# Splitting the pooling and delta branch inputs inside the last attention batch of a two-layer hybrid decoder step

## The chip, the cores and the metric

The kernel runs on one core of one Trainium2 chip. The metric is device microseconds (us) of one execution of the whole program, median of three runs. A core has five engines that take their instructions in order and wait for each other through semaphores: PE (the matrix multiplier TensorE), DVE (VectorE), ACT (ScalarE), POOL (GpSimd) and SP (SyncE), which here only issues transfers from main memory. In the trace, PEld is PE's load of the stationary operand, which runs beside its matmuls.

## What is computed

Two layers of a decoder; 256 prompt tokens and 8 sample rows of 8 tokens, so 320 token columns, with a cached past of 2048 positions for each sample row. What matters here, cut from the reference:

```python
y_a = y_pool * silu(z_pool)               # causal pooling, 512 channels
o_lat = _mla_attend(q_lat, q_rope, keys_lat, keys_rope, pos, k_pos)
o_mla = einsum('blhc,chd->blhd', o_lat, w_uv).reshape(B, L, MLA_WIDTH)
y_b = o_mla * silu(z_mla)                 # attention, 512 channels
y_c = _rmsnorm(o_dn, dn_norm_g) * silu(z_dn)   # gated delta rule, 512 channels
gates = sigmoid(h_gate).reshape(B, L, N_BRANCH, D_MODEL)
merged = (gates[:, :, 0] * (y_a @ w_br_pool) + gates[:, :, 1] * (y_b @ w_br_mla)
          + gates[:, :, 2] * (y_c @ w_br_dn))
x = x + merged @ w_out                    # 1024 -> 1024
```

## The kernel before

Everything is held channels by tokens: a tile is 128 channels by 320 columns. Products in full precision are done as three fp32r matmuls: a weight tile is loaded into `wraw` (four buffers, SP's queue), ACT copies its high half to `wh` (L196), DVE subtracts to get the low half `wl` (L197), and `mm3` multiplies high by high (L220), high by low (L221) and low by high (L222) for each block of 128 input channels. The activations are split in the same way: `yH` by ACT (L202), `yL` by DVE (L203). The inputs of the three branches stand in `zs`: entries 0 to 3 pooling, 4 to 7 attention, 8 to 11 delta. A branch product `br` for one of eight output blocks m is 4 blocks of input channels, so 12 matmuls; a gate product `gate` has 8 blocks, so 24. In the text, product (n, m) is branch n (0 pooling, 1 the delta branch, 2 attention, in the order in which the loops run) and output block m. The table `branches` in the code holds, for each n, the gate number, the weight and the first entry of `zs`.

A layer goes through its projections, convolutions and the delta rule (with a triangular solve, L760 to L770, on DVE), then attention over the cached past of the sample rows, one row (batch, `bb`) after another, then the branch products, and `w_out` (`wo`). In the loop over `bb`, a batch takes the scores `sc` (PE, L1166), softens them (DVE maximum L1185, ACT exponential L1196), runs a gate product on PE beside that, combines the batch before (`olat`), transposes the weights (`PT` for the past, `PTn` for the own tokens), multiplies them with the cached values (`attend`: 32 `pv` matmuls L1237 and the own part L1241), and scales the result into `o` on ACT (L1243). The loop stands in a manual schedule: PE, DVE, ACT and POOL run it in the order in which it is written. All that stands behind the loop is placed by the compiler's automatic scheduler, which may move it forward into the loop's last batches; SP's transfers are always placed by it.

Behind the loop stand the split of the pooling branch (`split_y(p3a, 0)`, the last line in the manual schedule), product (0, 0), the last combination, in the second layer the last gate product, product (0, 1), and `oml`, which multiplies the combined attention by `w_uv`. Then the pools of the attention are closed, the pool `p3` opens, the delta and attention inputs are split (L202, L203), the residual `xT` is loaded (POOL queue, L1449, 1280 KB), and the other 22 products run by pairs of output blocks, each followed by its use: `acc` (L1327) for branch 0, `gt` (L1329) and a sum on POOL (L1330) for the two others. Gate results that were put aside in main memory come back on POOL's queue (L1316). In PSUM, the attention has four banks of the tag A, which `gate`, `olat`, `PT`, `PTn`, `pv`, `br` and `oml` take in turn: a matmul into a bank waits until the bank's last reader is done.

Of the kernel before, what the change touches and what calls it, by code (L numbers as in the profile page):

```python
# [11 lines left out]
F32 = mybir.dt.float32  # L12
F32R = mybir.dt.float32r
I32 = mybir.dt.int32
AF = mybir.ActivationFunctionType
# [4 lines left out]
DM, TP, TS, T = 1024, 256, 64, 320  # L20
# [96 lines left out]
def trunk(tc, I, O, layers=2):  # L117
# [292 lines left out]
    for l in range(layers):  # L410
# [896 lines left out]

        def split_y(pool, y0):
            yb[y0] = (pool.tile([128, 4, T], F32R, name=f"yH{y0}"), pool.tile([128, 4, T], F32R, name=f"yL{y0}"))
            for i in range(4):  # L1310
                split_x(yb[y0][0][:, i, :], yb[y0][1][:, i, :], zs[y0 + i])

        def branch(n, m, tag):
            if (n, m) in spilled:
                t = per.tile([128, T], F32, tag="gt", name="gt", bufs=NG)
                nc.gpsimd.dma_start(t, spilled[n, m])  # L1316
            else:
                if (n, m) not in early:
                    gate("pj")
                t = early[n, m]  # L1320
            _, wname, y0 = branches[n]
            w = split_w(load_w(I[wname][l][:, m * 128 : m * 128 + 128], 4, 128)[:, :4, :], 4)
            b = ps(tag, "br")
            mm3(b[:, :T], w, yb[y0], 4)
            if n == 0:
                accs[m] = p3a.tile([128, T], F32, tag="acc", name="acc", bufs=4)
                stt(accs[m], t, 1.0, b[:, :T], add, mult)  # L1327
            else:
                stt(t, t, 1.0, b[:, :T], add, mult)  # L1329
                nc.gpsimd.tensor_tensor(accs[m], accs[m], t, add)  # L1330


        with tc.manual_schedule(engines={mybir.EngineType.PE, mybir.EngineType.DVE, mybir.EngineType.Activation, mybir.EngineType.Pool}):
# [18 lines left out]
            for h in range(11):  # L1352
# [20 lines left out]
                if 3 <= h < 8:  # L1373
                    flip(0, keys, parts_[h - 3])
            phc.close()
            pb = pbc.enter_context(tc.tile_pool(name=f"pb_{l}", bufs=1, side="right", reuse_waits="tile"))
            gs = [gate_w() for _ in range(GL[0])]
# [4 lines left out]
            for bb in range(NB):  # L1382
                more = bb + 1 < NB
                S = soften(bb, sc, mx)
                if more:
# [4 lines left out]
                if more:  # L1390
                    flip(bb + 1, keys, 1)
                g = [(gs[0][0], gate_mm("A", gs[0][1]))]
                if o is not None:
# [11 lines left out]
                if two:  # L1405
                    gate_mm("A", gs[1][1], b, (4, 8))
                    gate_out(gs[1][0], b, bb < 6)
                weigh(bb, mx)
                o = attend(bb, PT, PTn, mx)
                if more:  # L1410
# [6 lines left out]
            wuv = load_wuv(pb.tile([128, 1024], F32, tag="S", name="wuv", bufs=2))  # L1417
            pdc.close()
            p3e = ExitStack()
            p3a = p3e.enter_context(tc.tile_pool(name=f"p3a_{l}", bufs=1, reuse_waits="tile"))  # L1420
            yb = {}
            split_y(p3a, 0)
        branch(0, 0, "A")
        combined(NB - 1, combine(o))
        if order:
            gate("A")
        branch(0, 1, "A")
        b = ps("A", "oml")
# [5 lines left out]
        for p in range(4):  # L1434
            stt(zs[4 + p][:, TP:], b[:, p * 64 : p * 64 + 64], 0.5, zs[4 + p][:, TP:], mult, mult)
        pbc.close()
        p2b.close()
        p2c.close()
        pec.close()


        last = l == layers - 1
        p3c, p3 = enter(f"p3_{l}", dict(pj=2, A=6) if last else dict(pj=4, A=4))
        wcfg.update(pool=p3, n=2)
        split_y(p3, 8)
        split_y(p3, 4)
# [3 lines left out]
        for mp in range(4):  # L1450
            for n in range(3):
                for m in (2 * mp, 2 * mp + 1):
                    if n or m > 1:
                        branch(n, m, "A")
# [74 lines left out]
```

## Times and profile before

| what | value |
|---|---|
| time, median of 3 runs (lowest, highest) | 1063.83 us (1061.71, 1064.25) |
| the profiled execution's own time | 1066.27 us |
| its span, first to last instruction | 1064.5 us |
| mean granted TensorE clock | 0.962 |
| PE, DVE, ACT, POOL busy | 995.7, 725.8, 456.5, 338.0 us |
| end of attention, first layer (last batch's scores to the eighth branch product) | 446 to 479 us |
| the same of the second layer | 964 to 995 us |
| triangular solve of the second layer | 627 to 646 us |

A row of the timeline gives the start and duration of an instruction (or of a run of like ones, xN), its engine, line, tiles, and in brackets how long the engine had been idle and what it waited for. The durations are of the profiled execution. Matmuls overlap each other: the distance between their starts is what one costs.

### The profile page before, as it was taken

Reading aid. Unit: us, or ns where it says so; the run is one execution under the profiler, and the core shown is the slowest. Engines: PE = TensorE matmul, PEld = TensorE weight load, DVE = VectorE, ACT = ScalarE, POOL = GpSimd, SP = SyncE. Lnnn points to the kernel's source line nnn. Section 1 sums busy time; section 2 is a strip of 40 time slices with the busy share of each in tenths; the row PEclk is TensorE's granted clock in tenths of the full one; section 3 lists DMA queues with packets and bytes.
Section 4 is the critical chain, followed back from the end, with each engine's and each line's share of the span. In section 5 each row is a group of like instructions: output and inputs, shape, how many; then the busy total and the mean of one; then the engine's idle time right before and its main releaser. Section 6 shows DMA issues by size and latency. Waiting matters only on the chain.

```text
span 1064.5 us, 24733 instructions
## 1 busy us (share of the span) xinstructions
PE 995.7 (94%) x10179; PEld 866.4 (81%) x10179; DVE 725.8 (68%) x1387; ACT 456.5 (43%) x810; POOL 338.0 (32%) x469
## 2 busy tenths in 40 slices
PE   8988899999979999989989979999998899999996
PEld 6877798987857888779978868999876678777996
DVE  3999884558676666558748988656666657574872
ACT  5663353543433333334545624336344333334453
POOL 3666221215151101025445542211335211100641
PEclk8999899999989999999998989999998899999998
DMA  8532333733645776258663332355255376742961
GB/s 231 155 97 80 100 92 84 206 95 106 190 139 158 237 242 222 96 154 233 158 200 79 101 99 70 101 153 141 71 162 182 102 254 211 248 157 83 278 169 50
DMA packets 202697, 159.22 MB, mean 150 GB/s; under 512 B 27704, under 2 KB 191826, under 8 KB 200010
## 3 DMA queue, kind: packets, MB, share of 16 engines
q1 hardware_dynamic: 176364, 98.47, 34.1%
q0 software_dynamic: 7424, 48.75, 13.0%
q10 hardware_dynamic: 18798, 10.44, 3.4%
q8 instruction: 80, 1.31, 0.5%
q14 instruction: 31, 0.25, 0.1%
HBM read 144.17 MB, written 13.68 MB: 148 GB/s over the span
## 4 chain that ended last, share of the span: by engine, by line
PE 71%; DVE 15%; ACT 5%; issue 3%; DMA 3%; POOL 1%; ACTq 0%; SPq 0%; DVEq 0%; POOLq 0%
PE sc L1166 6%; PE pv L1237 5%; PE gate L220 5%; PE pj L220 5%; PE pj L222 5%; PE gate L222 4%; PE pj L221 4%; PE gate L221 4%; DVE cy L505 4%; PE br L220 3%; PE br L221 2%; DVE wl L197 2%; PE br L222 2%; PE wo L220 2%; PE wo L222 2%
## 5 line engine op out<-in xcount | busy, mean ns | idle before, releaser
L196 ACT ACTIVATE wh<-wraw 128x1024 fp32r<-128x1024 f32 (+1 forms) x180 | 166.4, 935 | 174.3 <-PE pj L221 93.0
L197 DVE TENSOR_TENSOR wl<-wraw,wh 128x1024 fp32r<-128x1024 f32 (+2 forms) x165 | 187.9, 1147 | 69.2 <-ACT wh L196 68.2
L220 PE MATMUL pj<-xnH,wh 128*128 128x320 f32 (+1 forms) x528 | 174.7, 331 | 13.5 <-DVE V L497 7.6
L222 PE MATMUL pj<-xnH,wl 128*128 128x320 f32 (+1 forms) x528 | 172.3, 326 | 6.7 <-DVE wl L197 6.4
L221 PE MATMUL pj<-xnL,wh 128*128 128x320 f32 (+1 forms) x528 | 170.0, 322 | 0.0
L220 PE MATMUL gate<-xnH,wh 128*128 128x320 f32 x384 | 124.7, 325 | 1.5 <-DVE V L497 1.5
L222 PE MATMUL gate<-xnH,wl 128*128 128x320 f32 x384 | 120.5, 314 | 1.8 <-DVE wl L197 1.3
L220 PEld LDWEIGHTS pj<-xnH,wh 128*128 128x128 f32 (+1 forms) x528 | 103.4, 196 | 21.1 <-ACT wh L196 6.9
L221 PE MATMUL gate<-xnL,wh 128*128 128x320 f32 x384 | 119.4, 311 | 0.0
L222 PEld LDWEIGHTS pj<-xnH,wl 128*128 128x128 f32 (+1 forms) x528 | 103.1, 195 | 11.6 <-DVE wl L197 7.8
L221 PEld LDWEIGHTS pj<-xnL,wh 128*128 128x128 f32 (+1 forms) x528 | 103.3, 196 | 3.2 <-issue 1.8
L220 PEld LDWEIGHTS gate<-xnH,wh 128*128 128x128 f32 x384 | 72.8, 190 | 9.6 <-issue 6.3
L1156 DVE STREAM_TRANSPOSE KT<-kv 128x1024 f32<-128x1024 f32 x64 | 78.6, 1228 | 0.6
L222 PEld LDWEIGHTS gate<-xnH,wl 128*128 128x128 f32 x384 | 72.7, 189 | 3.3 <-DVE wl L197 1.8
L221 PEld LDWEIGHTS gate<-xnL,wh 128*128 128x128 f32 x384 | 72.8, 190 | 1.1 <-issue 0.8
L220 PE MATMUL br<-yH,wh 128*128 128x320 f32 x192 | 60.3, 317 | 5.7 <-ACT wh L196 1.9
L1237 PE MATMUL pv<-kv,PT 128*64 128x256 f32 x512 | 58.8, 382 | 2.3 <-ACT PT L1215 2.3
L1166 PE MATMUL sc<-KT,q 32*64 32x256 f32 x2048 | 59.9, 380 | 0.0
L221 PE MATMUL br<-yL,wh 128*128 128x320 f32 x192 | 59.6, 313 | 0.0
L222 PE MATMUL br<-yH,wl 128*128 128x320 f32 x192 | 59.1, 313 | 0.0
L505 DVE SCALAR_TENSOR_TENSOR cy<-V,prm,cy 128x344 f32<-128x344 f32 x72 | 56.5, 804 | 0.5
L1166 PEld LDWEIGHTS sc<-KT,q 32*64 32x64 f32 x2048 | 45.8, 132 | 12.7 <-issue 6.2
(406 smaller groups left out, 2055.2 us busy)
## 6 DMA issues: line engine op xcount, KB each, us to landing
wraw<-in_w_in SPq DMA_DIRECT2D x114, 512.0 KB
wraw<-in_w_out SPq DMA_DIRECT2D x16, 512.0 KB
q<-q4d SPq DMA_DIRECT2D x64, 72.0 KB
gate<-gt ACTq DMA_DIRECT2D x28, 160.0 KB
gt<-gate POOLq DMA_DIRECT2D x28, 160.0 KB, 3.6
wraw<-in_w_br_pool SPq DMA_DIRECT2D x16, 256.0 KB
wraw<-in_w_br_dn SPq DMA_DIRECT2D x16, 256.0 KB
wraw<-in_w_br_mla SPq DMA_DIRECT2D x16, 256.0 KB
```

The costliest lines, as they stand in the source:

```text
L196: act(h, raw, AF.Copy)
L197: (nc.gpsimd.tensor_tensor if spare or turn[0] in K["lo"] else tt)(lo, raw, h.bitcast(F32), sub)
L220: nc.tensor.matmul(out, wh[:, k, :], xh[:, first + k, :], start=k == 0, stop=False)
L221: nc.tensor.matmul(out, wh[:, k, :], xl[:, first + k, :], start=False, stop=False)
L222: nc.tensor.matmul(out, wl[:, k, :], xh[:, first + k, :], start=False, stop=k == nk - 1)
L505: stt(y, V[:, j : j + 344], wj(j), y, mult, add)
L1156: nc.vector.transpose(v[:, a], kv[:, a * 1024 : a * 1024 + 1024].rearrange("p (i k c) -> p i k c", i=4, k=8))
L1166: nc.tensor.matmul(sc[64 * hf : 64 * hf + 64, g, :256], q4[r, k, :], krT[r, keys_] if k == 8 else KT[r, k, keys_], start=k == 0, stop=k == 8,)
L1237: nc.tensor.matmul(pv[64 * hf : 64 * hf + 64, :256], PT[:, n * 128 + 64 * hf : n * 128 + 64 * hf + 64], kv[:, r : r + 256], start=n == 0, ...
```

## The change

The pool `p3a` opens at the start of the last batch (bb = 7), and ACT copies the high halves of the pooling inputs there, before the batch's exponential; DVE takes the low halves after its maximum, and the weight of product (0, 0) is split behind that. Product (0, 0) runs between the transposes and `attend`, and before `attend` the weight of (0, 1) and the delta inputs are split as well. Behind the loop, and now within the manual schedule, come the use of (0, 0), in the second layer the last gate product, (0, 1), the combination, the weights of both delta products, product (1, 0); then `oml` and (1, 1). Four products are then done when `p3` opens, where two were; `branch` is cut in three functions for it. The attention inputs are split in `p3` as before.

```diff
@@ -1305,29 +1305,47 @@
-        def split_y(pool, y0):
+        yb = {}
+
+        def split_hi(pool, y0):
             yb[y0] = (pool.tile([128, 4, T], F32R, name=f"yH{y0}"), pool.tile([128, 4, T], F32R, name=f"yL{y0}"))
             for i in range(4):
-                split_x(yb[y0][0][:, i, :], yb[y0][1][:, i, :], zs[y0 + i])
-
-        def branch(n, m, tag):
+                act(yb[y0][0][:, i, :], zs[y0 + i], AF.Copy)
+
+        def split_lo(y0):
+            for i in range(4):
+                tt(yb[y0][1][:, i, :], zs[y0 + i], yb[y0][0][:, i, :].bitcast(F32), sub)
+
+        def split_y(pool, y0):
+            split_hi(pool, y0)
+            split_lo(y0)
+
+        def branch_w(n, m):
+            wname = branches[n][1]
+            return split_w(load_w(I[wname][l][:, m * 128 : m * 128 + 128], 4, 128)[:, :4, :], 4)
+
+        def branch_mm(n, w, tag):
+            b = ps(tag, "br")
+            mm3(b[:, :T], w, yb[branches[n][2]], 4)
+            return b
+
+        def branch_out(n, m, b):
...
+        def branch(n, m, tag):
+            if (n, m) not in spilled and (n, m) not in early:
+                gate("pj")
+            branch_out(n, m, branch_mm(n, branch_w(n, m), tag))
...
@@ -1381,6 +1400,11 @@
             o = None
             for bb in range(NB):
                 more = bb + 1 < NB
+                if not more:
+
+                    pdc.close()
+                    p3a = p3e.enter_context(tc.tile_pool(name=f"p3a_{l}", bufs=1, reuse_waits="tile"))
+                    split_hi(p3a, 0)
                 S = soften(bb, sc, mx)
...
                 softened(bb, S, mx)
                 if more:
                     flip(bb + 1, keys, 1)
+                else:
+                    split_lo(0)
+                    w00 = branch_w(0, 0)
                 g = [(gs[0][0], gate_mm("A", gs[0][1]))]
...
+                if not more:
+                    b00 = branch_mm(0, w00, "A")
                 weigh(bb, mx)
+                if not more:
+                    w01 = branch_w(0, 1)
+                    split_y(p3a, 8)
                 o = attend(bb, PT, PTn, mx)
...
             wuv = load_wuv(pb.tile([128, 1024], F32, tag="S", name="wuv", bufs=2))
-            pdc.close()
-            p3e = ExitStack()
-            p3a = p3e.enter_context(tc.tile_pool(name=f"p3a_{l}", bufs=1, reuse_waits="tile"))
-            yb = {}
-            split_y(p3a, 0)
-        branch(0, 0, "A")
-        combined(NB - 1, combine(o))
-        if order:
-            gate("A")
-        branch(0, 1, "A")
+            branch_out(0, 0, b00)
+            if order:
+                gate("A")
+            b01 = branch_mm(0, w01, "A")
+            combined(NB - 1, combine(o))
+            w10 = branch_w(1, 0)
+            branch_out(0, 1, b01)
+            w11 = branch_w(1, 1)
+            branch_out(1, 0, branch_mm(1, w10, "A"))
         b = ps("A", "oml")
...
+        branch_out(1, 1, branch_mm(1, w11, "A"))
         pbc.close()
...
+        early_br = {(0, 0), (0, 1), (1, 0), (1, 1)}
...
-        split_y(p3, 8)
         split_y(p3, 4)
...
-                    if n or m > 1:
+                    if (n, m) not in early_br:
                         branch(n, m, "A")
```

What this does to PE's order at the end of the first layer's last batch: `PTn` is the last transpose, `pv` the products with the cached values, `br` a branch product, `olat` the last combination. Before:

```order
L1214 MATMUL PT<-cst,S 128x128 x8
L1223 MATMUL PTn<-cst,so 64x64
L1237 MATMUL pv<-kv,PT 64x256 x16
L1241 MATMUL pv<-cko,PTn 64x256
L220 MATMUL br<-yH_5293,wh 128x320
L1249 MATMUL olat<-cst,o 128x64 x2
L220 MATMUL br<-yH_5293,wh 128x320
```

and in the changed kernel, from the last matmuls of product (0, 0) to the first of (0, 1):

```order
L220 MATMUL br<-yH_5209,wh 128x320
L221 MATMUL br<-yL_5210,wh 128x320
L222 MATMUL br<-yH_5209,wl 128x320
L1237 MATMUL pv<-kv,PT 64x256 x16
L1241 MATMUL pv<-cko,PTn 64x256
L220 MATMUL br<-yH_5209,wh 128x320
L221 MATMUL br<-yL_5210,wh 128x320
```

A whole product now stands ahead of the `pv` matmuls, and the next follows them at once. On DVE, in the same batch, from the maximum to the copy of `PTn`, before:

```order
L1195 TENSOR_SCALAR mx<-mx 128x1
L1253 COPY olat<-olat 128x16x8
L460 TENSOR_TENSOR gt<-gate,rn 128x320
L197 TENSOR_TENSOR wl<-wraw,wh 128x512
L1224 COPY PTn<-PTn 64x64
```

and changed:

```order
L1195 TENSOR_SCALAR mx<-mx 128x1
L1317 TENSOR_TENSOR yL_5210<-zs,yH_5209 128x320 x4
L197 TENSOR_TENSOR wl<-wraw,wh 128x512
L1253 COPY olat<-olat 128x16x8
L460 TENSOR_TENSOR gt<-gate,rn 128x320
L1224 COPY PTn<-PTn 64x64
```

Four low halves and a weight's low half now stand ahead of the copy of `olat` and of the reading of the gate's bank (L460). On ACT, at the end of the second layer's last batch, where the last gate's weight is the tile of 1024 columns, before:

```order
L1197 ACTIVATE so,mx<-so,mx 64x64
L196 ACTIVATE wh<-wraw 128x1024
L461 ACTIVATE gt<-gt 128x320
L1215 ACTIVATE PT<-PT 128x512 x2
L1243 ACTIVATE o<-pv,mx 128x256
L202 ACTIVATE yH_11246<-zs 128x320 x4
```

and changed:

```order
L1197 ACTIVATE so,mx<-so,mx 64x64
L196 ACTIVATE wh<-wraw 128x512
L461 ACTIVATE gt<-gt 128x320
L1215 ACTIVATE PT<-PT 128x512 x2
L196 ACTIVATE wh<-wraw 128x512
L1313 ACTIVATE yH_11259<-zs 128x320 x4
L1243 ACTIVATE o<-pv,mx 128x256
L196 ACTIVATE wh<-wraw 128x1024
```

The last gate's weight is split behind `o` now, where the automatic scheduler had put it ahead of the transposes' copies. One more place has moved without a line of the diff on it: the automatic schedule of the second layer's opening, around its triangular solve. DVE there, before (X and R are steps of the solve, `z` and `U` read projections):

```order
L760 STREAM_SHUFFLE X_7137<-R 128x160
L761 TENSOR_TENSOR X_7137<-X_7137,a_6580 128x20x5
L762 TENSOR_TENSOR R<-R,X_7137 128x20x5
L760 STREAM_SHUFFLE X_7141<-R 128x160
L761 TENSOR_TENSOR X_7141<-X_7141,a_6580 128x20x6
L654 TENSOR_TENSOR z<-pj,rn 128x320
L762 TENSOR_TENSOR R<-R,X_7141 128x20x6
L760 STREAM_SHUFFLE X_7145<-R 128x160
```

and changed:

```order
L760 STREAM_SHUFFLE X_7137<-R 128x160
L654 TENSOR_TENSOR z<-pj,rn 128x320
L761 TENSOR_TENSOR X_7137<-X_7137,a_6580 128x20x5
L762 TENSOR_TENSOR R<-R,X_7137 128x20x5
L197 TENSOR_TENSOR wl<-wraw,wh 128x1024
L760 STREAM_SHUFFLE X_7141<-R 128x160
L657 SCALAR_TENSOR_TENSOR th<-th,z 128x320
L761 TENSOR_TENSOR X_7141<-X_7141,a_6580 128x20x6
L762 TENSOR_TENSOR R<-R,X_7141 128x20x6
L760 STREAM_SHUFFLE X_7145<-R 128x160
L626 TENSOR_TENSOR U<-pj,rn 128x256
```

The reading `z` of a projection stands two steps of the solve earlier, and the reading `U` of the next projection stands ahead of the solve's last step instead of behind its end.

## Rows read from the trace of the kernel before

**Rows 1.** Timeline of PE, end of the first layer's attention: start us, us, instruction.

```profile
450.88 0.24 PE L1223 MATMUL PTn<-cst,so 64*64 64x64 f32 x1
451.84 3.67 PE L1237 MATMUL pv<-kv,PT 128*64 128x256 f32 x32 [0.71 <-ACT PT L1215]
...
457.01 0.42 PE L220 MATMUL br<-yH,wh 128*128 128x320 f32 x1 [0.92 <-ACT yH L202]
...
464.81 0.41 PE L220 MATMUL br<-yH,wh 128*128 128x320 f32 x1 [1.92 <-DVE yL L203]
```

**Rows 2.** Timeline of DVE, same stretch.

```profile
450.32 0.48 DVE L460 TENSOR_TENSOR gt<-gate,rn 128x320 f32<-128x320 f32 x1
450.72 0.68 DVE L197 TENSOR_TENSOR wl<-wraw,wh 128x512 fp32r<-128x512 f32 x1
...
467.13 1.70 DVE L203 TENSOR_TENSOR yL<-zs,yH 128x320 fp32r<-128x320 f32 x4
```

**Rows 3.** Timeline of ACT, same stretch.

```profile
448.19 1.15 ACT L1196 ACTIVATE S<-S,mx 128x1024 f32<-128x1024 f32 x1 [4.84 <-DVE mx L1195]
...
449.91 0.63 ACT L196 ACTIVATE wh<-wraw 128x512 fp32r<-128x512 f32 x1
...
456.50 1.54 ACT L202 ACTIVATE yH<-zs 128x320 fp32r<-128x320 f32 x4
```

**Rows 4.** Timelines of SP and POOL (issues of loads), and of ACT behind them.

```profile
451.43 0.37 SPq L176 DMA_DIRECT2D wraw<-in_w_br_mla  x1
463.31 1.50 SPq L176 DMA_DIRECT2D wraw<-in_w_br_pool  x2
```

```profile
463.65 0.53 POOL L1449 DMA_DIRECT2D xT<-xs  x1
```

```profile
472.60 2.19 ACT L196 ACTIVATE wh<-wraw 128x512 fp32r<-128x512 f32 x4 [5.88 <-DMA wraw<-in_w_br_pool]
```

**Rows 5.** Slices: length, busy of PE, PEld, DVE, ACT, POOL, clock, DMA share, GB/s.

```profile
454.00:455.00 1.00, 1.00 (x13) 0.66 (x10) 0.00 (x0) 0.00 (x0) 0.00 (x0) 1.00 0.01 2
```

```profile
475.00:476.00 1.00, 1.00 (x6) 1.00 (x5) 1.00 (x2) 0.00 (x0) 0.70 (x2) 0.50 0.72 215
```

**Rows 6.** The page's part on DMA issues: KB each, us from issue to landing.

```profile
gt<-gate POOLq DMA_DIRECT2D x28, 160.0 KB, 3.6
```

**Rows 7.** Timeline of PE, the end of the sixth to the end of the eighth product.

```profile
471.80 0.31 PE L222 MATMUL br<-yH,wl 128*128 128x320 f32 x1
473.81 0.42 PE L220 MATMUL br<-yH,wh 128*128 128x320 f32 x1 [1.70 <-ACT wh L196]
...
479.07 0.31 PE L222 MATMUL br<-yH,wl 128*128 128x320 f32 x1
```

**Rows 8.** Timelines of PE, ACT and DVE, end of the second layer's attention.

```profile
974.77 0.42 PE L220 MATMUL br<-yH,wh 128*128 128x320 f32 x1 [0.92 <-ACT yH L202]
...
981.11 1.20 PE L1433 MATMUL oml<-olat,wuv 128*64 128x64 f32 x32
...
994.73 0.31 PE L220 MATMUL br<-yH,wh 128*128 128x320 f32 x1
```

```profile
967.65 1.06 ACT L196 ACTIVATE wh<-wraw 128x1024 fp32r<-128x1024 f32 x1
```

```profile
973.89 0.47 ACT L1243 ACTIVATE o<-pv,mx 128x256 f32<-128x256 f32 x1 [3.85 <-PE pv L1241]
```

```profile
968.75 1.23 DVE L197 TENSOR_TENSOR wl<-wraw,wh 128x1024 fp32r<-128x1024 f32 x1 [0.21 <-ACT wh L196]
```

**Rows 9.** Timelines of DVE and PE, triangular solve of the second layer.

```profile
639.06 0.49 DVE L654 TENSOR_TENSOR z<-pj,rn 128x320 f32<-128x320 f32 x1 [1.06 <-PE pj L222]
...
642.10 2.19 DVE L768 TENSOR_TENSOR TS<-R,cst 128x512 f32<-128x512 f32 x3
644.22 0.41 DVE L626 TENSOR_TENSOR U<-pj,rn 128x256 f32<-128x256 f32 x1
```

```profile
645.52 1.00 PE L793 MATMUL Y<-TS,ATm 64*64 64x32 f32 x28 [0.88 <-DVE TS L770]
```

More of the change, by code (lines that the diff above doesn't have):

```diff
@@ L1317, in branch @@
             else:
-                if (n, m) not in early:
-                    gate("pj")
                 t = early[n, m]
[L1321 to L1324, printed above, removed]
             if n == 0:
@@ L1375, in trunk @@
             phc.close()
+            p3e = ExitStack()
             pb = pbc.enter_context(tc.tile_pool(name=f"pb_{l}", bufs=1, side="right", reuse_waits="tile"))
```

## The prediction

> **What bounds the kernel now.** I read the table of engines first, then the list of what PE waits for, stretch by stretch, then the timelines of PE, ACT and DVE side by side around the places the change touches. PE is busy for most of the span, and nearly all branch products follow each other without a gap: 48 matmuls lie between 464.81 [rows 1] and 471.80 [rows 7], 0.146 us each, so a product of 12 costs 1.76 and a gate of 24 costs 3.5. Where PE works like this, moving a product gains nothing. Only waits can be won, and a wait that is won in one place may come back behind it. In the first layer PE waits 0.92 for the first pooling high half and 1.92 for the delta low halves [rows 1], then 1.70 for a weight split [rows 7]. After that last wait the granted clock was half, 0.50 or 1.2 GHz, for about three slices [rows 5]; after the 1.92 it was not. In the second layer the 0.92 is there again [rows 8], and the other two are nearly gone. So the change has most to win in the first layer.
>
> **First layer, ahead of the `pv` products.** ACT's four high halves take 1.54 [rows 3]. They go into its idle 4.84 before the exponential [rows 3]: cost nothing, since PE is on the scores and the gate, and if the cover were gone the exponential would be up to 1.5 late. DVE's four low halves take 1.70 and a weight's low half 0.68 [rows 2]. DVE ends its maximum at about 448.1, so the low halves end at 449.8; ACT's `wh` ends at 450.5 as before [rows 3], and DVE's `wl` at about 451.3. Only then come the copy of `olat` and L460, which before ended at 450.80 [rows 2] and now ends at about 452.0. What is queued behind it on DVE is the copy of `PTn`; who waits is PE, since `PTn` takes the bank that L460 reads. So `PTn` starts at 452.05 instead of 450.88 [rows 1], the 12 matmuls of product (0, 0) run to 454.0, and `pv` starts there, 2.16 later than 451.84 [rows 1] for 1.76 of work moved ahead: a loss of 0.4, the price of the DVE order. The wait of 0.71 for the copies of `PT` is hidden under the product.
>
> **First layer, behind them.** Before, PE was through `pv` at 456.09, which is 457.01 less its wait of 0.92 [rows 1], 4.25 after `pv` began. Now that is 458.25. Product (0, 1) follows at once, because its inputs are there, and covers the scaling of `o`; it ends at 460.0. `olat` takes 0.4 and `oml` 1.2 [rows 8] with some 0.2 for the copy between them, and the two delta products take 3.5, so PE is through four products at 465.4. Before, 24 matmuls from 464.81 [rows 1] ended at 468.3. The lead is 2.9.
>
> Next is the attention branch, whose first matmul needs a bank that is free only when DVE has used product (1, 1), and this use stands on DVE behind the low half of the third pooling weight. That weight's load can be issued when DVE has split the first delta weight, at about 461.4, where before its pair was issued from 463.31 [rows 4]. Uncaught, a load of this size takes about 2.6: the one issued at 451.43 [rows 4] had moved by 454, when the DMA share falls to 0.01 [rows 5]. The page gives 3.6 for a smaller load on POOL's queue [rows 6]. With `wh` 0.63, `wl` 0.68 and the use 0.48 [rows 2, 3], PE goes on between 465.8 and 467.0. I take 467.0, since the residual `xT` is loaded at the same time and so the 3.6 is the nearer row: a wait of 1.6. Four products more are 7.0, and I leave 0.6 for the fourth pooling weight: the layer's 96th branch matmul ends at 474.6. Before, it began at 479.07 [rows 7] and ended at 479.2. From there PE runs without waits, so the lead is kept. **Gain 4.6.** Ends: 5.8 if the load takes 2.6, and 2.7 if the clock falls after the new wait, as follows.
>
> What a fall of the clock costs is in rows 7: 24 matmuls from 473.81 to 479.2 took 5.4 where 3.5 is the price at full clock, so 1.9. The wait in question is a little shorter than the 1.70 that was followed by a fall and than the 1.92 that was not [rows 1, 7]; I take none. The Trainium skill, page "TensorE: Matmul & The Clock Gate", section Part 1 on the clock gate, says that a monitor of PE's activity halves the clock of an idle engine and gives it back to a busy one. The trace agrees after the 1.70, with its 0.50, and shows nothing of it after the 1.92. With a fall after both new waits, this one and the second layer's, the whole sum below would be +3.0; with none after either, −0.8.
>
> **Second layer, end of attention.** The delay of 0.4 on DVE is the same. The removed wait is 0.92 [rows 8]. New is the last gate: before, its weight was split beside the transposes (`wh` 1.06 from 967.65, `wl` 1.23 from 968.75 [rows 8]) and cost PE nothing. Now ACT splits it behind `o`, which itself starts when `pv` is done and takes 0.47 [rows 8]. PE has nothing else in its order there, since the next instruction is the gate's first: it waits 0.47 + 1.06 and about 0.25 of hand-over, 1.8, does two matmuls, and waits about 1.0 more for the low half. From 974.77 to the 96th branch matmul at 994.73 [rows 8] there are 20.1 us for 96 + 24 matmuls (17.6), `oml` (1.2) and `olat` (0.4), so 0.9 of small waits, which the earlier inputs may remove. That makes 1.8 + 1.0 + 0.4 − 0.92 − 0.9 = 1.4 lost. Two idle stretches of together 2.8, close to each other, are more than the 1.70 before the one fall I can see here, so I add 1.9. **Loss 3.3**, ends 1.4 and 4.2 (none of the 0.9 won).
>
> **Second layer, opening.** No line of the diff stands here, but the order has moved, and DVE runs in order. Before, DVE was idle 1.06 until the projection for `z` was there at 639.06 [rows 9]. Now `z` stands two steps of the solve earlier, so those steps wait for the same projection instead of running before it, and `U`, which read its projection at 644.22 [rows 9], behind the solve's end, now stands ahead of its last step. TS, three instructions of 2.19 that began at 642.10 [rows 9], then begin at about 646.7, and `Y`, which waits for them through two transposes, at 650.1 instead of 645.52 [rows 9]: 4.6 later. What PE is given in between is 22 projection matmuls and a transpose, 3.5 us that stood behind `Y` before. If all that follows is bound by PE, 1.1 is lost; if it hangs on `Y`, 4.6; and if the solve's end is waited for elsewhere anyway, nothing. PE waits for DVE here (0.88 before `Y` [rows 9]), so it is not PE alone: I take 2.4. **Loss 2.4**, ends 0 and 4.6.
>
> **The sum.** −4.6 + 3.3 + 2.4 = +1.1 on the profiled execution's 1066.27: 1067.4. The median of the runs shown is 2.4 below that execution, so 1064.9. Other moves (transfer issues one product earlier, pools that open earlier) lie beside PE's work.
>
> **Rivals.** *Faster.* The solve's new order costs nothing because its fillers are needed soon anyway, the load comes in 2.6 (gain 5.8), and the clock holds at the last gate (loss 1.4): −4.4, 1059.4. For it: the scheduler gives PE work in the gap. Against it: three things have to go well at once. Chance 0.14.
>
> *Slower by a caught load.* The third pooling weight's load shares the transfer engines with `xT`, 1280 KB, issued on POOL's queue at 463.65, 0.3 after the pair's issue began [rows 4]; the splits of the pair came at 472.60 [rows 4], 9.3 after it. If that happens to the load now, the wait before the attention branch grows to about 7 us, product eight ends at about 479.4, and the first layer wins nothing: 3.3 + 2.4 = +5.7, 1069.5. It decides if the load's data has not moved before `xT` starts. Against it: `xT` waits for `oml`, so it starts a microsecond or more after the load's issue. Chance 0.17. The Trainium skill, page "DMA: Bandwidth & Descriptors", section Queues, rings and completion order, says that a transfer engine takes turns between its queues, a packet at a time; with turns of equal bytes the load would take twice its 2.6, and the sum would be +2.7, but the 9.3 shows much less than an equal share.
>
> *Slower by the solve.* The opening costs its full 4.6 and the clock falls also after the first layer's new wait (gain 2.7): 4.6 + 3.3 − 2.7 = +5.2, 1069.0. For it: DVE's chain is what PE waits for there. Chance 0.14.
>
> **How the numbers follow.** My forecast has 0.55; its own range is 1061.4 to 1066.9. About 0.3%, 3.2 us, is what a measurement of this kernel can tell from no change; the forecast lies inside it. So faster 0.14, same 0.55, slower 0.31. The range leaves out about 0.1 at each end: 1060.2 to 1069.6.
>
> **What would show it.** Right: no wait of PE for `yH` or delta `yL` in the first layer, `pv` some 2.2 later and (0, 1) directly behind it; a wait of 1.5 or less at the first attention product; PE idle twice on `wh` and `wl` of the last gate in the second layer, with a clock near 0.5 behind; `Y` of the second solve further from the layer's start by some 2 to 5 us. Wrong: a gate weight that is split in time after all, a load that comes after 470, or a solve whose `Y` is not later.

## The result, and the profile after

The changed kernel takes 1071.43 us (median of 5 runs, 1070.81 to 1072.89); the kernel before took 1064.04 beside it (5 runs, 1061.71 to 1066.63). The ratio is 1.0073 with the interval 1.0057 to 1.0089: slower by about 7.4 us, outside the predicted range. A second set of runs on another chip gave 1.0056 (1.0038 to 1.0073).

The profiled execution of after took 1071.43, that of before 1066.27, so 5.2 lie between the two traces. Measured from span start, the first layer's 96th branch matmul begins 3.6 earlier than before, the first `Y` of the second layer's solve 0.5 later, and the second layer's first `wo` matmul 5.3 later (its 96th branch matmul 4.9). The start of the program (no change there) accounts for −0.15 of the first. So the first layer's end won 3.4, 3.1 of it behind the last `sc`; the opening of the second layer lost 4.1; and its end lost 4.7, of which 4.2 lie ahead of the 96th branch matmul.

Busy times are those of before within 4 us (share of the span, instructions):

```profile
PE 998.9 (93%) x10179; PEld 868.5 (81%) x10179; DVE 724.7 (68%) x1387; ACT 457.3 (43%) x810; POOL 337.4 (32%) x469
```

**End of the first layer's attention**, PE's timeline of after; it answers to [rows 1] and [rows 7]:

```profile
451.15 0.21 PE L1223 MATMUL PTn<-cst,so 64*64 64x64 f32 x1 [0.66 <-DVE olat L1253]
451.55 0.38 PE L220 MATMUL br<-yH,wh 128*128 128x320 f32 x1 [0.18 <-DVE gt L460]
...
453.47 3.67 PE L1237 MATMUL pv<-kv,PT 128*64 128x256 f32 x32
457.07 0.64 PE L1241 MATMUL pv<-cko,PTn 64*64 64x256 f32 x2
457.64 0.41 PE L220 MATMUL br<-yH,wh 128*128 128x320 f32 x1
...
466.99 0.38 PE L220 MATMUL br<-yH,wh 128*128 128x320 f32 x1 [1.94 <-DVE gt L1342]
```

The waits of 0.92 and 1.92 in [rows 1] are gone, product (0, 1) starts directly behind `pv` at 457.64, and PE is through four products at 465.1. Then it waits 1.94 for a bank, until DVE has used product (1, 1). That use stands behind the third pooling weight's low half, which needs ACT's high half, which needs the load; DVE's and ACT's rows of after show the chain backwards, and SP's and POOL's the issues ([rows 4] of before):

```profile
465.76 0.69 DVE L197 TENSOR_TENSOR wl<-wraw,wh 128x512 fp32r<-128x512 f32 x1 [0.64 <-ACT wh L196]
466.37 0.48 DVE L1342 SCALAR_TENSOR_TENSOR gt<-gt,br 128x320 f32<-128x320 f32 x1
...
465.09 1.15 ACT L196 ACTIVATE wh<-wraw 128x512 fp32r<-128x512 f32 x2 [1.39 <-DMA wraw<-in_w_br_pool]
469.62 0.63 ACT L196 ACTIVATE wh<-wraw 128x512 fp32r<-128x512 f32 x1 [3.38 <-DMA wraw<-in_w_br_pool]
...
461.01 1.37 SPq L176 DMA_DIRECT2D wraw<-in_w_br_pool  x2
462.20 0.53 POOL L1481 DMA_DIRECT2D xT<-xs  x1
```

The third pooling weight, issued at 461.01, is split at 465.09, 4.1 later. The fourth, the second issue of the same row, begins at 462.01, 0.2 ahead of `xT`, and is split at 469.62, 7.6 later. The clock fell behind the 1.94. In the slices of after (PE, PEld, DVE, ACT and POOL busy, then granted clock, DMA share, GB/s) one stands for it:

```profile
468.00:469.00 1.00, 1.00 (x6) 1.00 (x5) 0.00 (x0) 0.00 (x0) 0.70 (x2) 0.50 1.19 318
```

**Opening of the second layer**, DVE and PE of after, against [rows 9]:

```profile
635.50 0.49 DVE L654 TENSOR_TENSOR z<-pj,rn 128x320 f32<-128x320 f32 x1 [2.35 <-PE pj L222]
...
639.67 0.41 DVE L626 TENSOR_TENSOR U<-pj,rn 128x256 f32<-128x256 f32 x1
642.97 1.62 DVE L768 TENSOR_TENSOR TS<-R,cst 128x512 f32<-128x512 f32 x3
...
645.99 1.81 PE L793 MATMUL Y<-TS,ATm 64*64 64x32 f32 x54
```

DVE waits 2.35 for `z`'s projection where it waited 1.06, and `U` stands ahead of the TS instructions. `Y` begins at 645.99; before it was 645.52, but there the first layer had ended 3.6 later.

**End of the second layer's attention**, PE and ACT of after, against [rows 8]:

```profile
978.08 0.41 PE L220 MATMUL gate<-xnH,wh 128*128 128x320 f32 x1 [1.51 <-ACT wh L196]
...
979.33 0.63 PE L222 MATMUL gate<-xnH,wl 128*128 128x320 f32 x1 [0.70 <-DVE wl L197]
...
976.61 0.47 ACT L1243 ACTIVATE o<-pv,mx 128x256 f32<-128x256 f32 x1 [2.93 <-PE pv L1241]
976.98 1.05 ACT L196 ACTIVATE wh<-wraw 128x1024 fp32r<-128x1024 f32 x1
...
996.75 0.63 ACT L196 ACTIVATE wh<-wraw 128x512 fp32r<-128x512 f32 x1 [5.29 <-DMA wraw<-in_w_br_pool]
```

ACT scales `o` first, since it stands ahead of the gate's weight in the new order; PE waits 1.51 for the high half and 0.70 for the low one. The fourth pooling weight comes late here too, and here PE waits for it; its issue (the second of the first row), that of `xT`, and PE's first wait for it:

```profile
987.46 1.37 SPq L176 DMA_DIRECT2D wraw<-in_w_br_pool  x2
988.66 0.53 POOL L1481 DMA_DIRECT2D xT<-xs  x1
...
997.44 0.41 PE L220 MATMUL br<-yH,wh 128*128 128x320 f32 x1 [0.31 <-ACT wh L196]
```

Behind the gate's two waits the clock is at half, one of the slices of after:

```profile
981.00:982.00 1.00, 1.00 (x6) 1.00 (x5) 0.00 (x0) 0.00 (x0) 0.00 (x0) 0.50 0.41 120
```

### The profile page after: what moved, and what is told of

It reads as the page before. It is cut to its first block, busy times and chain, and to the rows that moved or that the text cites. A ratio compares the mean times of both kernels' runs of the same rounds, so it can differ in the third digit from the quotient of the medians.

```text
span 1069.5 us, 24731 instructions
## 1 busy us (share of the span) xinstructions
PE 998.9 (93%) x10179; PEld 868.5 (81%) x10179; DVE 724.7 (68%) x1387; ACT 457.3 (43%) x810; POOL 337.4 (32%) x469
## 4 chain that ended last, share of the span: by engine, by line
PE 67%; DVE 18%; ACT 6%; issue 3%; DMA 3%; POOL 1%; ACTq 0%; SPq 0%; DVEq 0%; POOLq 0%
PE sc L1166 6%; PE pv L1237 5%; PE gate L220 5%; PE pj L220 5%; PE pj L222 4%; PE gate L222 4%; DVE cy L505 4%; PE pj L221 4%; PE gate L221 4%; DVE wl L197 3%; PE br L220 2%; PE br L222 2%; PE br L221 2%; PE wo L220 2%; PE wo L222 2%
## 5 line engine op out<-in xcount | busy, mean ns | idle before, releaser
L220 PE MATMUL br<-yH,wh 128*128 128x320 f32 x192 | 60.8, 317 | 2.8 <-DVE gt L1342 1.9
```

Source lines behind the costliest of these rows:

```text
L220: nc.tensor.matmul(out, wh[:, k, :], xh[:, first + k, :], start=k == 0, stop=False)
```

## Experiments

All runs are compared over the same four stretches, cut by PE's instructions so that nothing ahead of them counts: **A**, from the first layer's last `sc` matmul to its first `wo`; **B**, from the second layer's first norm matmul to the first `Y` of its solve; **D**, from that `Y` to the second layer's last `sc`; **C**, from there to its first `wo`. Each is one distance in one profiled execution, in us:

| kernel | order of the opening | A | clock fell in A | B | D | C |
|---|---|---|---|---|---|---|
| before | before's | 61.79 | yes | 109.98 | 317.81 | 59.70 |
| after | new | 58.68 | yes | 114.03 | 317.98 | 64.40 |
| after_again | new | 57.10 | no | 111.04 | 317.23 | 63.66 |
| e1_l0 | new | 57.54 | no | 111.95 | 319.99 | 59.69 |
| e2_l1 | before's | 59.85 (before's code) | yes | 107.15 | 318.10 | 64.56 |
| e3_pin | pinned | 57.75 | no | 111.57 | 323.19 | 64.39 |
| e4_hoist | new | 57.34 | no | 113.29 | 318.29 | 60.88 |
| e5_order | before's | 58.95 | yes | 107.06 | 317.85 | 64.18 |
| e6_xlate | new | 59.00 | yes | 112.84 | 317.84 | 64.12 |
| e7_all | before's | 57.64 | no | 107.97 | 317.80 | 60.30 |
| e7_again | before's | 58.94 | yes | 107.74 | 320.24 | 60.34 |
| e9_bank | before's | 61.94 | yes, twice as long | 110.05 | 321.93 | 63.85 |
| e10_ho | before's | 57.76 | no | 108.16 | 318.09 | 61.87 |
| e11_bank_x | before's | 57.35 | no | 107.35 | 318.42 | 60.38 |

The theory was the prediction's: a gain at the first layer's end, a loss at the second's through the late weight of the last gate, and a loss in the opening through the order of the solve. The rivals: each of these may be nothing, and the residual's load may be behind what was not won.

**One layer alone.** In e1_l0 the second layer's end is written as in before, in e2_l1 the first layer's; both have the edit below in the places that the diff touches, with `l == 0` or `l == 1`.

```diff
+        new = l == 0
...
-                if not more:
+                if new and not more:
```

> The change in the first layer alone; the second layer keeps the old order behind its attention. On every engine the opening of the second layer, around the triangular solve, stands in the order of the changed kernel. Theory (three separate terms, read from the two traces: first layer -3.4 us, solve +4.1, end of the second layer +4.7): -3.4 + 4.1, so about +0.7 us against before, with Y of the second layer's solve some 4 us further from the layer's start than before. Rival (the losses of the second layer hang together, and nothing is lost at the solve once its end is undisturbed): -3.4 us.

Measured: 1068.52 against 1066.72 for before, run beside it (as in every run below), ratio 1.0016 (0.9997 to 1.0035), so +1.7. A is won, C is before's to 0.01, and B is 111.95: gain and loss in the opening come together. The rival's −3.4 falls.

> The change in the second layer alone; the first layer and the opening of the second stand as in the kernel before. Theory of three separate terms: only the end of the second layer is lost, +4.7 us against before (+3.2 if the weight loads behind it are not caught by the residual's load this time), with PE idle about 2.2 us at the last gate's weight halves and the clock at 0.5 behind it. Rival (that end costs only because the layer before shifted it in time): within 1 us of before.

Measured: 1070.82 against 1066.72, ratio 1.0036 (1.0014 to 1.0059), so +3.8. PE's row at the last gate has the wait again:

```profile
976.03 0.41 PE L220 MATMUL gate<-xnH,wh 128*128 128x320 f32 x1 [1.51 <-ACT wh L196]
```

C is 64.56, 4.9 longer than in before. The rival that it is nothing falls. The run also gave something that wasn't asked for: its B, with before's order, is 2.8 shorter than in before's own trace, and its first layer, before's code too, shows no wait of 1.70 for a weight, which [rows 7] has, and a fall of the clock behind the wait of 1.9, where before has none. One trace doesn't give these distances to better than 2 or 3 us.

**The opening.** e3_pin ties `z` and `U` to steps of the solve by hand (`z`'s lines; `U`'s are alike):

```diff
-            tt(z, b, rn, mult)
+            with tc.issue_after(done8[2].ins) if l and g == 0 else ExitStack():
+                tt(z, b, rn, mult)
```

> The changed kernel with two instructions of the second layer's opening tied down: the reading z of the first pooling gate behind the sixth step's product of the solve, as in the kernel before, and the reading U of the second pooling projection behind the third TS, as in the kernel before. A few instructions further on, in the delta rule, move too. Theory (the order on DVE makes Y late): Y comes about 4 us earlier than in the changed kernel and the whole is 2.5 to 4 us faster than it, +3.5 to +5 against before. Rival (the loss there comes from the time at which the layer starts, not from the order): as the changed kernel, +7 against before.

Measured: 1075.8 against 1066.72, ratio 1.0093 (1.0066 to 1.0121): not faster, if anything slower. DVE's rows show that the place of `z` was taken by a weight, and behind the solve PE waits in the delta rule:

```profile
633.90 1.23 DVE L197 TENSOR_TENSOR wl<-wraw,wh 128x1024 fp32r<-128x1024 f32 x1 [1.95 <-ACT wh L196]
...
648.83 1.41 PE L648 MATMUL mix<-d,mixw 128*128 128x320 f32 x2 [2.42 <-DVE d L646]
```

The scheduler placed what stands around the two instructions anew, and PE still has the new order, with 22 more projection matmuls ahead of `Y` than before (408 against 386), so this run doesn't tell what the order costs. e5_order does it from the other side: one line of the last attention batch is written a few lines later, and the scheduler's order of the opening is then before's.

```diff
                     split_lo(0)
-                    w00 = branch_w(0, 0)
...
                 gate_out(*g[0], bb < 6)
+                if not more:
+                    w00 = branch_w(0, 0)
```

> The changed kernel with the split of the weight of product (0, 0) written behind the use of the gate product in the last batch, where it stood ahead of it: ACT's wh and DVE's wl move two and three places in either layer. The automatic order of the second layer's opening comes out, with it, as in the kernel before, through the whole triangular solve (PE differs from it by where two mix products stand, DVE by z standing one group later behind the solve). The last batches should run within 0.5 us of the changed kernel. Theory (the solve's order on DVE costs 4 us): 3.5 to 4.5 us faster than the changed kernel, Y of the solve less than 0.5 us later in relation to the layer's start than in the kernel before. Rival (the solve is later because the layer starts at another time, the order costs nothing): within 1 us of the changed kernel.

Measured: 1066.88 against 1063.59, ratio 1.0042 (1.0021 to 1.0064), where after had 1.0056 beside it. The trace has the order and the B that were expected: `z` waits 0.45, TS begin earlier, and B is 107.06 against 111.0 and 114.0 of after's two traces.

```profile
634.43 0.49 DVE L654 TENSOR_TENSOR z<-pj,rn 128x320 f32<-128x320 f32 x1 [0.45 <-PE pj L222]
637.46 2.19 DVE L768 TENSOR_TENSOR TS<-R,cst 128x512 f32<-128x512 f32 x3
...
640.89 1.00 PE L793 MATMUL Y<-TS,ATm 64*64 64x32 f32 x28 [0.88 <-DVE TS L770]
```

The time followed by less than expected (2.9 by the medians, 1.5 by the ratios, whose intervals overlap). The table settles the stretch itself: eight traces with before's order have B between 107.1 and 110.1 (mean 108.2), five with the new one between 111.0 and 114.0 (mean 112.6). The ranges don't meet; the order makes `Y` 4.5 later. That alone isn't yet a loss, since the 22 matmuls, some 3.2 us at 0.146 each, now lie in B and no longer behind it. But D is no shorter for it: 318.3 in the mean of the five, 318.8 of the eight. So the loss lasts: from the norm to the last `sc` (B and D together) the means are 430.9 and 427.0, 4 us apart. Without e9_bank, whose traced execution was the slowest of its twelve, the ranges are 428.3 to 432.0 and 424.9 to 428.0.

**The last gate.** e4_hoist splits the gate's weight with the first pooling weights, ahead of `attend`; one ACT and one DVE instruction move.

```diff
                     w01 = branch_w(0, 1)
+                    gl = gate_w() if order else None
...
-            if order:
-                gate("A")
+            if gl:
+                gate_out(gl[0], gate_mm("A", gl[1]))
```

> The changed kernel with the last gate's weight of the second layer split ahead of the delta inputs, before the pv products; against the changed kernel one instruction on ACT and one on DVE have moved, nothing else. Theory (PE idle 2.2 us for the two halves and the fall of the clock behind that idle time, 1.5 to 1.9): 3.5 to 4 us faster than the changed kernel, with no low clock between 975 and 985 us. Rival (the idle time alone counts, the clock falls in any case): 2.2 faster. Second rival (the wait comes back at the next product, whose load is late): under 1 faster.

Measured: 1068.2 against 1066.72, ratio 1.0013 (0.9994 to 1.0032). PE's waits from 960 to 1030 (us in total, times, longest) are these; none is for the gate:

```profile
PE PTn L1223 <- DVE olat L1253: 0.7, 1, 0.7
PE br L220 <- ACT wh L196: 0.5, 2, 0.3
PE br L222 <- DVE wl L197: 0.3, 2, 0.2
PE br L220 <- DVE gt L460: 0.2, 1, 0.2
```

The six traces with the late weight have C between 63.7 and 64.6 (mean 64.2), each with a fall of the clock; this one has 60.9 without a fall, 3.3 less for waits of 2.2. The rest agrees with the clock, which no longer falls here.

**After once more**, for the comparison beside e5_order, e6_xlate and e7_all:

> The changed kernel once more, on the same chip as the next three, to compare them with it directly. +7 us against before, as in its first comparison (1.0073); every theory expects that.

Measured: 1069.79 against 1063.59, +6.2. Its profiled execution took 1066.42, its median is 3.4 above that, and the clock does not fall in A: the same program, another execution.

**The residual's load.** e6_xlate issues `xT` behind the sum of product (2, 1), the instruction on POOL that the edit calls `summed[2, 1]`:

```diff
-        nc.gpsimd.dma_start(xT, xs[l])
         for mp in range(4):
+            if mp == 1:
+                with tc.issue_after(summed[2, 1].ins):
+                    nc.gpsimd.dma_start(xT, xs[l])
```

> The changed kernel with the load of the residual issued behind the sum of product (2, 1) on POOL, about 8 us later; PE's order is unchanged. Theory (the 256 KB pooling weights are caught behind the 1280 KB of the residual): the loads' splits come 3 us earlier, PE's wait of 1.94 us at the first attention product of the first layer shrinks below 1 and the clock stays at 1 behind it, and the 1.5 us lost from the seventh to the ninth product of the second layer go: 2.5 to 4 us faster than the changed kernel. Rival (the loads are late because SP issues them late, the residual does not matter): within 1 us.

Measured: 1069.27 against 1063.59, ratio 1.0052 (1.0031 to 1.0074): no gain over after. ACT's and PE's rows, and the two issues, tell why:

```profile
465.84 1.15 ACT L196 ACTIVATE wh<-wraw 128x512 fp32r<-128x512 f32 x2 [1.74 <-DMA wraw<-in_w_br_pool]
467.14 0.63 ACT L196 ACTIVATE wh<-wraw 128x512 fp32r<-128x512 f32 x1 [0.15 <-DMA wraw<-in_w_br_pool]
...
467.74 0.61 PE L220 MATMUL br<-yH,wh 128*128 128x320 f32 x1 [2.28 <-DVE gt L1342]
...
461.41 1.37 SPq L176 DMA_DIRECT2D wraw<-in_w_br_pool  x2
475.61 0.54 POOL L1484 DMA_DIRECT2D xT<-xs  x1
```

With `xT` out of the way the fourth pooling weight, issued at 462.41, is split 4.7 after its issue instead of 7.6, but the third still takes 4.4, and that is the one PE waits for. So the residual does not hold up the third load; it does hold up the fourth, for which nobody waits here as long as the bank is late. In the second layer PE does wait for the fourth, and there the later `xT` moves the loss: from the last `sc` to the 96th branch matmul PE takes 34.6 where after takes 35.6, but from there to the first `wo` 29.5 instead of 28.8. The Trainium skill, page "DMA: Bandwidth & Descriptors", section Queues, rings and completion order, has a transfer engine take turns between its queues, a packet at a time; the fourth weight's 2.9 agrees with a delay by another queue's packets, and the third weight, issued 1.2 ahead of `xT`, shows none of it (4.1 with `xT` beside it, 4.4 without).

**The two cures, with and without the later `xT`.** e10_ho is e4_hoist and e5_order together; e7_all and its repetition e7_again are e10_ho and e6_xlate.

> The changed kernel with the last gate's weight split ahead of the delta inputs and the weight of product (0, 0) behind the use of the gate product; the residual's load stays where the changed kernel has it. Theory (the residual's load catches only a load that is not needed yet): within 1 us of the kernel with all three, so as fast as before within 2 us. Rival (that load counts): 2 us slower than with all three.

> All three together: the last gate's weight split ahead of the delta inputs, the weight of product (0, 0) behind the use of the gate product, the residual's load behind the sum of product (2, 1). If the three causes are separate their gains add: 4 + 4 + 3, so about 10 us faster than the changed kernel and 3 us faster than before. Rival (they are one chain of which each takes the same part): 4 to 5 faster than the changed kernel, 2 to 3 slower than before.

> The kernel with all three once more, on the same chip as the run before it, for a direct comparison: within 1 us of before, as in its first comparison (1.0007).

Measured: e10_ho 1064.83 against 1065.63, ratio 0.9997 (0.9975 to 1.0019); e7_all 1063.25 against 1063.59, 1.0007 (0.9990 to 1.0024); e7_again 1067.05 against 1066.55, 1.0016 (1.0000 to 1.0031). Against after's 1.0073 and 1.0056 the two cures bring back 4 to 8 us, with or without the later load; the gain of A that should then remain is not seen in the time. In the table B is before's, and C is 60.3 to 61.9.

**The bank's wait.** e9_bank is e10_ho with the third pooling weight tied behind DVE's use of (1, 1); e11_bank_x has the later `xT` as well.

```diff
+                used[n, m] = stt(t, t, 1.0, b[:, :T], add, mult)
...
+            with tc.issue_after(used[1, 1].ins) if (n, m) == (0, 2) else ExitStack():
+                w = branch_w(n, m)
+            branch_out(n, m, branch_mm(n, w, tag))
```

> The next kernel (hoisted gate split and the order of the first batch weight) with one thing more: DVE's low half of the third pooling weight is tied behind the use of product (1, 1), so that the first attention product's PSUM bank is freed without waiting for that weight's load. Theory (PE's wait of about 2 us there comes from the bank, held by that order on DVE, and the fall of the clock behind it): PE begins the attention products within 0.5 us of the end of the delta products, the first layer's end is 2 us shorter (4 with the fall), the second's under 0.5: 2 to 4 us faster than the next kernel, 1060 to 1062. Rival (the attention products then wait for their weights or inputs instead): within 0.5 us of the next kernel.

Measured: 1069.94 against 1065.63, ratio 1.0040 (1.0020 to 1.0061), 4.6 slower by the ratios than e10_ho beside it. The traced execution is the slowest of the twelve (1076.17). PE's rows have the two waits, ACT's the load that was caught:

```profile
468.04 0.39 PE L220 MATMUL br<-yH,wh 128*128 128x320 f32 x1 [0.67 <-DVE gt L1342]
473.31 0.63 PE L220 MATMUL br<-yH,wh 128*128 128x320 f32 x1 [2.69 <-ACT wh L196]
...
472.63 0.63 ACT L196 ACTIVATE wh<-wraw 128x512 fp32r<-128x512 f32 x1 [4.48 <-DMA wraw<-in_w_br_pool]
```

The wait of 1.9 falls to 0.67, and the next one, 2.69 for the fourth pooling weight, comes up in its place with another fall of the clock: A is 61.94.

> Both at once: the bank freed early as in the run with the tied low half, and the residual's load behind the sum of product (2, 1), with the hoisted gate split and the order of the first batch weight. Theory (at the end of the first layer two waits stand one behind the other, the bank's and, hidden behind it, that of the fourth pooling weight caught by the residual's load): PE's waits there together below 1.2 us, the stretch from the last batch's scores to w_out 55.5 to 56.5 us where it was 57.1 to 59.0 in the changed kernel, no fall of the clock; 2 us faster than the kernel with all three, 3 faster than before. Rival (the weights cannot come faster, since their loads wait for a free wraw buffer): as the kernel with all three.

Measured: 1064.72 against 1066.55, ratio 0.9984 (0.9965 to 1.0003), the best of all versions, 2.3 by the medians below e7_again on the same chip (2 were expected), and still not to be told from before. The caught load is gone, but PE now waits for a high half in the bank's place:

```profile
467.14 0.38 PE L220 MATMUL br<-yH,wh 128*128 128x320 f32 x1 [1.27 <-ACT wh L196]
```

A is 57.35, where 55.5 to 56.5 was expected, and PE's waits there come to 2.3 instead of less than 1.2: bank, weight and residual wait one behind the other, so each edit uncovers the next.

## Why the prediction was wrong

The mechanisms were mostly the predicted ones, and the two likely losses were named with the right sign and place. Four sizes were off, all to the same side; the time is 6.5 above the forecast, 4.1 of it in the sum and 2.4 in the base.

- **The base.** "The median of the runs shown is 2.4 below that execution, so 1064.9." This step took it that the new kernel's executions lie below its sum as those of before lie below theirs. Before's profiled execution was 2.4 above the median of its kernel; after's was at its median. It is the largest single error. What failed, as far as it can be read, is that terms of an execution above the median (a wait of 1.70 with a fall of the clock behind it, [rows 5, 7]) were counted as gains in full, and the same excess was then taken off once more. e2_l1, with before's code in its first layer and without the 1.70, speaks for it; there is no second trace of before to show it.
- **The first layer: gain 3.4 between the two profiles instead of 4.6.** Each instant up to the bank's wait was right to 0.9: `PTn` 451.15 (forecast 452.05), `pv` 453.47 (454.0), four products through at 465.1 (465.4), PE on again at 466.99 (467.0), a wait of 1.94 (1.6). The 466.99 is partly luck: the third weight's load was issued 0.4 earlier than forecast (461.01, not 461.4) and was there 4.1 after its issue, not 3.6. The step that failed is "I take none" for a fall of the clock: it fell, inside the stated end of 2.7. Over the ten traces that have the change here and not the bank's edit, the clock fell in four (A 58.7 to 59.0) and held in six (57.1 to 57.8), so a fall costs 1.4, and neither choice was safe. Their mean, 58.1, is 2.7 less than the mean of the two traces with before's code (61.79 and 59.85): that is the gain to be expected of an execution at large, since the 1.70 is not in each execution of before's code.
- **The opening: loss 4.1 instead of 2.4.** The failed step is "it is not PE alone: I take 2.4", the middle between 1.1 or nothing and 4.6. The upper end was nearly right: the TS instructions, forecast 4.6 later, began 4.4 later counted from the layer's norm matmul, and the projections that PE does in the gap gave nothing back. The groups of traces show it, 4.5 apart in B and 4 in B and D together. Which later instruction hangs on `Y` was not measured by itself. The working has `z` "two steps of the solve earlier"; the order printed under the change shows it one step earlier, in the step of X_7137 instead of that of X_7141.
- **The second layer's end: loss 4.7 instead of 3.3.** The waits of 1.51 and 0.70 came to 2.2 (forecast 2.8) and the fall of the clock was there. The failed step is the 0.9 of small waits "which the earlier inputs may remove". In before's trace only 0.24 of it, at 984.21, is a wait of PE, so there was little to remove; and a new wait came up, for the fourth pooling weight, issued beside `xT` and split only at 996.75. From 997.44 to 1002.72 PE's matmuls begin 1.5 later than at 0.146 each, 1.0 of it ahead of the 96th branch matmul, where the forecast ends, and 0.5 behind. Up to that matmul the loss is 4.2. The forecast with the 0.9 left in gives 4.2 as well, but with other terms. e1_l0 and e2_l1 show that the whole of the loss belongs to this layer's edit. The gate's weight is 3.5 of it: that much lies between the means of C in the six traces with the late weight and in the five that have it early and no fall of the clock (64.2 and 60.8; 61.3 with e9_bank, which has it early too and whose clock fell further on).

Of the rivals, the slower one by a caught load was half true: the load that is caught is the fourth, hidden in the first layer by the bank's wait until that is taken away (e9_bank), and waited for in the second. The slower one by the solve, full 4.6 and a fall of the clock, is nearest to what happened, and its 1069.0 is short by 2.4, as much as was taken off for the base. That its sum of +5.2 is met is partly luck: its three terms are 4.6, 3.3 and −2.7 where 4.1, 4.7 and −3.4 were measured.

Open: with both cures the stretches add up to a gain (A −2.7, B 0, C +1.1, and some 0.3 to 0.9 more in `wo` where the load is late), yet the time is not below before's. Of the missing 1 to 3 us, 0.4 lie outside the span, in every run: an execution of before takes 1.7 to 1.9 longer than its span, one of e7_all, e7_again, e10_ho or e11_bank_x 2.2 to 2.3. D may hold some more (317.8 to 320.2 in the three traces with both cures, 317.8 in before's). The rest is within what single traces scatter, and no run tells where it lies. That e3_pin lost some 5 us behind its solve (D is 323.2) is read off its trace alone, and the cause stays open beyond the wait of 2.42.

## What to carry to other kernels

Where an automatic scheduler places the rest of the program, compare its order over the whole program after a local edit: here a stretch 160 us further on, without a line in the diff, moved and cost more than the edited place won. A weight split that is written behind a late instruction on an engine that runs in order is late itself, even if its load was issued long before (the gate's at 948.68, 28 us ahead of its split); written ahead of `attend` it cost PE no wait. Price a wait from more than one execution, and take the conversion from a profiled execution to a median as an uncertainty of its own and not as a term.

## What the runs showed of the hardware

- The same instructions don't take the same time. From the span's start to the first `sc`, which no change touches, the traces have 323.9 to 326.7 us, with 31 to 48 us of it at half the TensorE clock. One slice each of before and of e5_order, 0 to 320 us (PE, PEld, DVE, ACT and POOL busy, granted clock, DMA share, GB/s), shows 0.95 against 0.93 of the clock for like work:

```profile
0.00:320.00 320.00, 294.92 (x2703) 254.93 (x2703) 229.87 (x450) 146.76 (x258) 124.69 (x175) 0.95 0.48 131
```

```profile
0.00:320.00 320.00, 297.57 (x2700) 258.65 (x2700) 228.26 (x446) 145.86 (x253) 123.41 (x174) 0.93 0.48 131
```

- A wait of PE of about 1.9 was followed by the lower clock, 0.50 or 1.2 GHz, in some executions and not in others of one and the same program: after and after_again differ in that, and before's wait of 1.92 [rows 1] was not followed by a fall while e2_l1's of 1.9 at the same place was. The length of the wait doesn't decide it: over the ten traces with the change in the first layer and without the bank's edit, the clock fell behind 1.87 to 2.28 and held behind 1.87 to 2.55. The Trainium skill, page "TensorE: Matmul & The Clock Gate", section Part 1 on the clock gate, has the clock follow PE's activity; the rows shown here agree in that it falls behind waits, and they leave open behind which.
